# First input pieces on one DMA queue, blocks on two queues, 12 warming matmuls; indexer queries of the second chunk stacked by head pairs

## The chip, the cores and the metric

The kernel runs on one core of one Trainium2 chip. The metric is the device time of one execution in microseconds (us). The kernel before has a median of 431.6 us over 3 runs (431.47 to 431.8).

## The reference, cut to what matters

The kernel computes one step of a hybrid encoder layer for 256 prompt frames and 32 sample frames, 288 columns in all. Everything starts from one combined projection `p = x @ w_in`. The part that the second half of the change touches is the indexer of the sparse attention:

```
sc    = einsum('bqhd,bsd->bqhs', qi, ki) * IDX_DIM**-0.5      # 8 heads of 64, one shared key per frame
score = einsum('bqh,bqhs->bqs', wi * IDX_HEADS**-0.5, relu(sc))
adm   = arange(S) < (qpos // CHUNK + 1) * CHUNK               # CHUNK = 64: chunk-causal
score = where(adm, score, -inf)
_, idx = top_k(score, k_sel)                                  # k_sel = 64 for the 256 prompt frames
```

A prompt query in chunk 0 (frames 0 to 63) may use 64 keys, all of which it takes; one in chunk 1 (64 to 127) may use 128 keys; those in chunks 2 and 3 (128 to 255) up to 256 keys. Scores are thus needed for queries 64 to 127 against keys 0 to 127, and for queries 128 to 255 against keys 0 to 255.

## The kernel before, in words

Each projection tile is 128 output rows times 288 columns, summed over 8 blocks of 128 input rows. Every float32 operand is split into a high part (a cast to fp32r on ScalarE, `act.copy`) and a low part (a subtraction on VectorE), and each product is three fp32r matmuls: high by high, high by low, low by high.

The opening works block by block. The array `first` holds, for each input block k from 0 to 7, the 288 columns of x and the 128 weight columns of each of the first five tiles (0: the small tile with indexer key, gates and indexer weights; 1 to 4: the indexer queries): 928 columns, 464 KB. Block 0 is loaded in two pieces: `lead[0][:, 0:416]` (x and tile 0) on the queue of SP (line 161), the other 512 columns on the queue of ACT (line 162); blocks 1 to 7 follow on SP (line 164). For each block ACT casts `xh` (line 169) and `wh` (line 176), DVE subtracts `xl` (line 172) and `wl` (line 177). PE goes through the blocks in order (`first_products`, line 937): for block 0 three matmuls of tile 0, then 12 of tiles 1 to 4 with 224 columns each; for every later block 15, the first five of which need `wh` of that block. Ahead of them PE runs `WARM` = 18 matmuls on a zeroed tile (line 148), whose results nobody uses.

After the opening PE runs one tile after another (lines 899 to 901, 24 matmuls each), and a list of generators puts side work into the middle of each tile. ACT casts a tile's weights three tiles ahead, DVE subtracts two tiles ahead. All orders are fixed when the program is built; at run time engines only wait for semaphores.

The indexer queries of head pair j arrive as one tile of 128 rows (head 2j in rows 0 to 63, head 2j+1 in rows 64 to 127). `evac_qi` (lines 374 to 382) builds from them, for each head, a stationary operand `qst[:, h]` of 128 rows: high parts in the head's own half of the rows, low parts in the other half; `kih` and `kil` hold the key twice, so that one matmul with `kih` and one with `kil` give the full product. `index` (lines 384 to 404) then takes for each head queries 128 to 255 and queries 0 to 127, each against 256 keys, and ACT and DVE form relu and the weighted sum, with the weights `wn` (line 280).

Of the kernel before, what the change touches and what calls it, by code (L numbers as in the profile page):

```python
# [10 lines left out]
F32 = mybir.dt.float32  # L11
F32R = mybir.dt.float32r
BF = mybir.dt.bfloat16
AF = mybir.ActivationFunctionType
OP = mybir.AluOpType
# [5 lines left out]
TP = 256  # L21
TS = 32
T = TP + TS
KT = D // 128
AH, AD = 4, 256
BH, BD = 8, 128
IH, ID = 8, 64
CHUNK = 64
WARM = 18
MID = 4  # L30
FIRST = 5
LEAD = T + 128 * FIRST
# [8 lines left out]
NOT_ADMISSIBLE = -3.0e38  # L41
# [42 lines left out]
def body(ctx, tc, a, o):  # L84
    nc = tc.nc
    pe, act, dve, pool, sp = nc.tensor, nc.scalar, nc.vector, nc.gpsimd, nc.sync
# [5 lines left out]
    def sb(name, shape, dt=F32, tag=None, bufs=1):  # L92
        return P.tile(shape, dt, name=name, tag=tag or name, bufs=bufs)

    def bank(name, n=512):
        return ps.tile([128, 512], F32, name=name, tag="side", bufs=6)
# [24 lines left out]
    def pair(name):  # L121
        return (sb(f"wh{name}", [128, KT * 128], F32R, tag="wh", bufs=4),
                sb(f"wl{name}", [128, KT * 128], F32R, tag="wl", bufs=4))
# [18 lines left out]
    warm = sb("warm", [128, 256], BF)  # L142
# [3 lines left out]
    def keep_warm(n):  # L146
        for _ in range(n):
            pe.matmul(wp[:, :256], lhsT=warm[:, :128], rhs=warm, start=True, stop=True)

    keep_warm(WARM)  # L150

# [7 lines left out]
    lead = [sb(f"wst_k{k}", [128, KT * 128], tag="wst", bufs=8) for k in range(KT)]  # L159
    cut = T + 128  # L160
    sp.dma_start(lead[0][:, 0:cut], a["first"][:, 0, 0:cut])
    act.dma_start(lead[0][:, cut:LEAD], a["first"][:, 0, cut:])
    for k in range(1, KT):
        sp.dma_start(lead[k][:, 0:LEAD], a["first"][:, k])
    leads = []
    for k in range(KT):
        raw, (wh, wl) = lead[k], pair(f"_k{k}")
        leads.append((wh, wl))
        act.copy(xh[:, k], raw[:, 0:T])
        if k == 0:  # L170
            dve.tensor_copy(wh[:, 0:128], raw[:, T:cut])
        dve.tensor_tensor(xl[:, k], raw[:, 0:T], xh[:, k].bitcast(F32), OP.subtract)
        if k == 0:
            dve.tensor_tensor(wl[:, 0:128], raw[:, T:cut], wh[:, 0:128].bitcast(F32), OP.subtract)
        p = cut if k == 0 else T
        act.copy(wh[:, p - T:LEAD - T], raw[:, p:LEAD])
        dve.tensor_tensor(wl[:, p - T:LEAD - T], raw[:, p:LEAD], wh[:, p - T:LEAD - T].bitcast(F32), OP.subtract)
# [60 lines left out]
    start(8, bias_table())  # L238


    wn = sb("wn", [128, 3, 8])
    ws = sb("ws", [128, 2])
    gnat = sb("gnat", [128, 2, 3, 4])
    gns = sb("gns", [128, 3])
# [27 lines left out]
    def index_weights():  # L272
        sm = store["sm"]
        p = bank("wn_p")
        for b in range(2):
            pe.transpose(p[:, 128 * b:128 * b + 128], sm[:, 128 * b:128 * b + 128], ident)
        pe.transpose(p[:TS, 256:384], sm[:, TP:T], ident)
        c8 = float(np.float32(IH ** -0.5))
        for b in range(2):
            dve.tensor_scalar(wn[:, b], p[:, 128 * b + 68:128 * b + 76], c8, ID ** -0.5, op0=OP.mult, op1=OP.mult)  # L280
        dve.tensor_scalar(wn[:TS, 2], p[:TS, 256 + 68:256 + 76], c8, ID ** -0.5, op0=OP.mult, op1=OP.mult)
        yield
        for i in range(4):
            dve.tensor_copy(ws[32 * i:32 * i + 32], wn[:TS, 2, 2 * i:2 * i + 2])

    def gates():
        ig, z = store["ig"], store["z"]
# [77 lines left out]
            yield  # L365


    qst = sb("qst", [128, IH, TP], F32R, tag="cv")
    qis = sb("qis", [128, 4, TS])
    pool.memset(qst[:, :, 0:CHUNK].bitcast(F32), 0.0)  # L370
    kih = sb("kih", [128, TP], F32R, tag="hn", bufs=2)
    kil = sb("kil", [128, TP], F32R, tag="hn", bufs=2)

    def evac_qi(j, p):
        act.copy(qis[:, j], p[:, TP:T])
        new = slice(CHUNK, TP)
        half = (slice(0, 64), slice(64, 128))
        for e in range(2):
            act.copy(qst[half[e], 2 * j + e, new], p[half[e], new])
        for e in range(2):  # L380
            own, other, h = half[e], half[1 - e], 2 * j + e
            dve.tensor_tensor(qst[other, h, new], p[own, new], qst[own, h, new].bitcast(F32), OP.subtract)

    def index():
        acc = sb("acc", [128, 384], tag="sw", bufs=2)
        accs = sb("accs", [128, T], tag="sw", bufs=2)
        srel = [sb(f"srel{i}", [128, T], tag="ba", bufs=2) for i in range(2)]
        for j in range(IH // 2):
            p = [bank(f"ix{j}{e}") for e in range(2)]
            for e in range(2):  # L390
                h = 2 * j + e
                for c, q in ((0, slice(128, 256)), (256, slice(0, 128))):
                    pe.matmul(p[e][:, c:c + 256], lhsT=qst[:, h, q], rhs=kih, start=True, stop=False)  # L393
                    pe.matmul(p[e][:, c:c + 256], lhsT=qst[:, h, q], rhs=kil, start=False, stop=True)  # L394
            for e in range(2):
                h = 2 * j + e
                r = sb(f"r{h}", [128, 384], tag="lg", bufs=3)
                act.activation(r, p[e][:, :384], AF.Relu)
                w0, w1 = wn[:, 0, h:h + 1], wn[:, 1, h:h + 1]
                for c, w in ((slice(0, 256), w1), (slice(256, 384), w0)):  # L400
                    if h == 0:
                        dve.tensor_scalar(acc[:, c], r[:, c], w, None, op0=OP.mult)
                    else:
                        dve.scalar_tensor_tensor(acc[:, c], r[:, c], w, acc[:, c], op0=OP.mult, op1=OP.add)
            yield
            if j == 1:
                q = [bank(f"ixs{par}") for par in range(2)]
                for part in range(2):
                    for par in range(2):
                        r = slice(64 * par, 64 * par + 64)  # L410
                        c, keys = ((slice(0, 256), cki[r]), (slice(256, T), kiT[r, TP:T]))[part]
                        for i in range(4):
                            pe.matmul(q[par][32 * i:32 * i + 32, c], lhsT=qis[r, i], rhs=keys, start=True, stop=True)
                for par in range(2):
                    dve.tensor_scalar(srel[par], q[par][:, :T], 0.0, ws[:, par:par + 1], op0=OP.max, op1=OP.mult)
                dve.tensor_tensor(srel[0], srel[0], srel[1], OP.add)
            if j == 2:
                p = bank("ixsum")
                pe.matmul(p[:, :T], lhsT=stack, rhs=srel[0], start=True, stop=True)
                act.copy(accs, p[:, :T])  # L420
            yield
        dve.memset(acc[0:64, 256 + 64:384], NOT_ADMISSIBLE)
        dve.memset(acc[0:64, 192:256], NOT_ADMISSIBLE)
        top = sb("top", [128, 3, 8])
        for r in range(9):
            if r % 2:
                yield
            for i, (w, rows) in enumerate(((acc[:, 256:384], 128), (acc[:, 0:256], 128), (accs, 128))):
                if r == 8 and i < 2:
                    continue  # L430
                tt = top[:rows, i]
                dve.max(tt, w)
                dve.match_replace(w, tt, w, TAKEN)
            yield
        bm = store["bm"]
        dve.memset(acc[0:64, 256:256 + 64], TAKEN)
        mk = sb("mk", [128, 384], tag="lg", bufs=3)
        mks = srel[0]
        dve.tensor_scalar(mk, acc, TAKEN_LIMIT, MASK, op0=OP.is_gt, op1=OP.mult)
        dve.tensor_scalar(mks, accs, TAKEN_LIMIT, MASK, op0=OP.is_gt, op1=OP.mult)  # L440
        yield
        for h in range(0, 8, 2):
            dve.tensor_tensor(bm[:, h:h + 2], bm[:, h:h + 2], mk[:, None, :].to_broadcast([128, 2, 384]), OP.add)
            if h % 4 == 0:
                yield
        dve.tensor_tensor(bms, bms, mks[:, None, :].to_broadcast([128, 2, T]), OP.add)
        store["masked"] = True
# [7 lines left out]
    cv = sb("cv", [128, 2, D], tag="cv")  # L455
# [353 lines left out]
    def evac(t, p):  # L809
# [4 lines left out]
        if n == "sm":  # L814
            evac_small(p)
        elif n == "qi":
            evac_qi(j, p)
        elif n == "qb":
            act.copy(qbT[:, j], q)
# [208 lines left out]


    start(FIRST + 3, index())  # L1030
    s0 = POS["vb", 7] + 4
    start(s0 - 2, attn_sample())
# [18 lines left out]
    first = first_products()  # L1051
# [115 lines left out]
```

## Time and profile before

| what | value |
|---|---|
| median of 3 runs | 431.6 us |
| the profiled execution, its own time | 431.44 us |
| its span, first to last instruction | 429.7 us |
| PE busy | 422.5 us, 98% of the span |
| DVE busy | 299.2 us, 70% |
| ACT busy | 231.3 us, 54% |
| DMA, mean over the span | 183 GB/s |

The span leaves out 1.74 us of the execution's own time. A share of busy time is an average over stages; the opening, in which PE waits for data, is 1% of the span.

### The profile page before, as it was taken

The page shows a single profiled execution, that of the slowest core. Times are in us where ns is not written, and L with a number is a line of the kernel's source. Part 1 is how long each engine was busy: PE and PEld are TensorE (multiplying, and loading weights), DVE is VectorE, ACT ScalarE, POOL GpSimd, SP SyncE. Part 2 cuts the span into 40 slices and gives each one's busy share as a digit, 9 for nine tenths or more (in the row PEclk, how much of TensorE's full clock was granted, in tenths as well). Part 3 has the DMA queues.
Part 4 walks back from the last instruction along what each step waited for, and adds up shares of the span by engine and source line. Part 5 has one row for each costly group of instructions (what it writes and reads, how often), then busy time and mean ns, then how long its engine had stood idle before and what let it go on. Part 6 is the DMA issues. An engine that isn't in the chain of part 4 may idle for free.

```text
span 429.7 us, 8392 instructions
## 1 busy us (share of the span) xinstructions
PE 422.5 (98%) x3297; PEld 411.5 (96%) x3297; DVE 299.2 (70%) x598; ACT 231.3 (54%) x463; POOL 22.8 (5%) x44
## 2 busy tenths in 40 slices
PE   8999999999999999999999999999999999999994
PEld 7999999999999999999999999999999999998874
DVE  5779889886656664766999887776453465665674
ACT  6776456446665665557795465555433444446402
POOL 1000000000300000000001101101000000000031
PEclk9999999999999999999999999999999999999998
DMA  8986869968844455734454455554565558543014
GB/s 306 352 333 190 277 204 337 299 134 298 298 118 147 143 149 149 243 104 146 145 148 149 130 176 187 146 148 141 164 186 151 170 171 262 152 138 122 27 47 138
DMA packets 28707, 78.70 MB, mean 183 GB/s; under 512 B 7508, under 2 KB 10812, under 8 KB 27868
## 3 DMA queue, kind: packets, MB, share of 16 engines
q1 hardware_dynamic: 27804, 76.85, 57.4%
q10 hardware_dynamic: 864, 1.32, 0.9%
q8 instruction: 26, 0.43, 0.4%
q14 instruction: 13, 0.11, 0.1%
HBM read 72.39 MB, written 7.67 MB: 186 GB/s over the span
## 4 chain that ended last, share of the span: by engine, by line
PE 95%; DVE 2%; ACT 1%; DMA 1%; POOLq 0%; issue 0%; DVEq 0%; ACTq 0%
PE pj L900 25%; PE pj L899 25%; PE pj L901 25%; PE yn L918 5%; PE pj L937 3%; PE yn L922 1%; DMA wst_k<-in_first 1%; PE apt L569 1%; ACT wh L130 0%; PE al L550 0%; PE ix L394 0%; PE ix L393 0%; PE s L610 0%; PE av L579 0%; PE vt L623 0%; PE kt L664 0%
## 5 line engine op out<-in xcount | busy, mean ns | idle before, releaser
L899 PE MATMUL pj<-xh,wh 128*128 128x288 f32 x704 | 209.9, 298 | 0.1
L900 PE MATMUL pj<-xl,wh 128*128 128x288 f32 x704 | 207.7, 295 | 0.0
L901 PE MATMUL pj<-xh,wl 128*128 128x288 f32 x704 | 207.5, 295 | 0.0
L130 ACT CAST wh<-wst 128x1024 fp32r<-128x1024 f32 x112 | 117.8, 1052 | 132.3 <-PE pj L900 85.6
L137 DVE TENSOR_TENSOR wl<-wst,wh 128x1024 fp32r<-128x1024 f32 x112 | 136.4, 1219 | 32.3 <-ACT wh L130 31.9
L899 PEld LDWEIGHTS pj<-xh,wh 128*128 128x128 f32 x704 | 132.4, 188 | 0.9 <-issue 0.4
L900 PEld LDWEIGHTS pj<-xl,wh 128*128 128x128 f32 x704 | 132.4, 188 | 0.1
L901 PEld LDWEIGHTS pj<-xh,wl 128*128 128x128 f32 x704 | 132.3, 188 | 0.0
L899 PE MATMUL pj<-bbh,wh 128*128 128x288 f32 x64 | 19.1, 299 | 0.0
L900 PE MATMUL pj<-bbl,wh 128*128 128x288 f32 x64 | 19.0, 296 | 0.0
L900 PE MATMUL pj<-bal,wh 128*128 128x288 f32 x64 | 18.9, 295 | 0.0
L901 PE MATMUL pj<-bah,wl 128*128 128x288 f32 x64 | 18.9, 295 | 0.0
L901 PE MATMUL pj<-bbh,wl 128*128 128x288 f32 x64 | 18.8, 294 | 0.0
L899 PE MATMUL pj<-bah,wh 128*128 128x288 f32 x64 | 18.8, 293 | 0.0
L918 PE MATMUL yn<-wh,mxh 128*128 128x512 f32 x32 | 13.0, 407 | 0.0
L918 PE MATMUL yn<-wl,mxh 128*128 128x512 f32 x32 | 12.7, 396 | 0.1
L918 PE MATMUL yn<-wh,mxl 128*128 128x512 f32 x32 | 12.6, 394 | 0.0
L899 PEld LDWEIGHTS pj<-bbh,wh 128*128 128x128 f32 x64 | 12.1, 188 | 0.0
L901 PEld LDWEIGHTS pj<-bbh,wl 128*128 128x128 f32 x64 | 12.0, 188 | 0.0
L899 PEld LDWEIGHTS pj<-bah,wh 128*128 128x128 f32 x64 | 12.0, 188 | 0.0
L900 PEld LDWEIGHTS pj<-bal,wh 128*128 128x128 f32 x64 | 12.0, 188 | 0.0
L901 PEld LDWEIGHTS pj<-bah,wl 128*128 128x128 f32 x64 | 12.0, 188 | 0.0
(466 smaller groups left out, 567.8 us busy)
## 6 DMA issues: line engine op xcount, KB each, us to landing
wst<-in_w SPq DMA_DIRECT2D x112, 512.0 KB, 3.7
wst_k<-in_first SPq DMA_DIRECT2D x7, 464.0 KB, 4.8
rscr<-rrow SPq DMA_DIRECT2D x2, 768.0 KB, 6.8
out_k<-kbT SPq DMA_DIRECT2D x1, 1152.0 KB, 8.1
stC<-in_state_C SPq DMA_DIRECT2D x1, 1028.0 KB
out_C_sample<-stC SPq DMA_DIRECT2D x1, 1028.0 KB
bm<-rscr SPq DMA_DIRECT2D x1, 1024.0 KB, 7.6
ckT<-in_cache_k SPq DMA_DIRECT2D x1, 1024.0 KB
```

The lines of the kernel that those rows point to most:

```text
L130: act.copy(split[t][0], stage[t])
L137: dve.tensor_tensor(wl, stage[t], wh.bitcast(F32), OP.subtract)
L569: pe.transpose(p[:, 128 * i:128 * i + 128], lg[:, c:c + 128], ident)
L899: pe.matmul(p[:, :T], lhsT=wh[:, c], rhs=h[:, k], start=(k == 0), stop=False)
L900: pe.matmul(p[:, :T], lhsT=wh[:, c], rhs=l[:, k], start=False, stop=False)
L901: pe.matmul(p[:, :T], lhsT=wl[:, c], rhs=h[:, k], start=False, stop=(k == KT - 1))
L918: pe.matmul(p, lhsT=x[:, k, r], rhs=w[:, c], start=first and i == 0, stop=last and i == 2)
L922: pe.matmul(p[32 * q:32 * q + 32, 0:256], lhsT=lazy["mxs"][:, k], rhs=stage[t][:, 256 * q:256 * q + 256], start=first, stop=last)
L937: pe.matmul(p[t][:, new], lhsT=w[:, 128 * t:128 * t + 128], rhs=x[:, k, new], start=(k == 0 and w is wh and x is xh), stop=(k == KT - 1 an ...
```

## The change

In the opening, the second piece of block 0 moves from ACT's queue to SP's, right behind the first piece. Blocks 1, 3, 5 and 7 stay on SP; blocks 2, 4 and 6 go to ACT's queue: 2 and 4 behind a one-column copy named `tick`, 6 behind the cast of `xh` of block 1. The warming matmuls are 12 instead of 18.

In the indexer, a pair of heads now shares one stationary operand for the queries of chunk 1: `qst[:, j]` holds 128 columns for head 2j (queries 128 to 255), 128 columns with queries 64 to 127 of both heads side by side, and 128 columns for head 2j+1. The shared operand goes against keys 0 to 127 only. Its output rows 0 to 63 belong to head 2j, rows 64 to 127 to head 2j+1; they are weighted with `wp0` and the two halves are added at the end through the tile `odd`.

```diff
-WARM = 18
+WARM = 12
...
     sp.dma_start(lead[0][:, 0:cut], a["first"][:, 0, 0:cut])
-    act.dma_start(lead[0][:, cut:LEAD], a["first"][:, 0, cut:])
-    for k in range(1, KT):
-        sp.dma_start(lead[k][:, 0:LEAD], a["first"][:, k])
+    sp.dma_start(lead[0][:, cut:LEAD], a["first"][:, 0, cut:])
+    act.copy(sb("tick", [128, 1], BF), warm[:, 0:1])
+
+    def lead_load(q, k):
+        q.dma_start(lead[k][:, 0:LEAD], a["first"][:, k])
+
+    for k in (1, 3, 5, 7):
+        lead_load(sp, k)
+    for k in (2, 4):
+        lead_load(act, k)
...
+        if k == 1:
+            lead_load(act, 6)
         p = cut if k == 0 else T
         act.copy(wh[:, p - T:LEAD - T], raw[:, p:LEAD])
...
-        for b in range(2):
-            dve.tensor_scalar(wn[:, b], p[:, 128 * b + 68:128 * b + 76], c8, ID ** -0.5, op0=OP.mult, op1=OP.mult)
-        dve.tensor_scalar(wn[:TS, 2], p[:TS, 256 + 68:256 + 76], c8, ID ** -0.5, op0=OP.mult, op1=OP.mult)
+        dve.tensor_scalar(wn[:, 0], p[:, 128 + 68:128 + 76], c8, ID ** -0.5, op0=OP.mult, op1=OP.mult)
+        dve.tensor_scalar(wn[:TS, 1], p[:TS, 256 + 68:256 + 76], c8, ID ** -0.5, op0=OP.mult, op1=OP.mult)
+        for e in range(2):
+            dve.tensor_scalar(wp0[64 * e:64 * e + 64], p[64:128, 68 + e:76:2], c8, ID ** -0.5, op0=OP.mult, op1=OP.mult)
...
-    qst = sb("qst", [128, IH, TP], F32R, tag="cv")
+    qst = sb("qst", [128, IH // 2, 384], F32R, tag="cv")
-    pool.memset(qst[:, :, 0:CHUNK].bitcast(F32), 0.0)
...
-        for e in range(2):
-            act.copy(qst[half[e], 2 * j + e, new], p[half[e], new])
-        for e in range(2):
-            own, other, h = half[e], half[1 - e], 2 * j + e
-            dve.tensor_tensor(qst[other, h, new], p[own, new], qst[own, h, new].bitcast(F32), OP.subtract)
+        parts = [(e, slice(t0, t1), slice(c, c + t1 - t0))
+                 for e, t0, t1, c in ((0, 64, 128, 128), (0, 128, 256, 0), (1, 64, 256, 192))]
+        for e, new, c in parts:
+            act.copy(qst[half[e], j, c], p[half[e], new])
+        for e, new, c in parts:
+            own, other = half[e], half[1 - e]
+            dve.tensor_tensor(qst[other, j, c], p[own, new], qst[own, j, c].bitcast(F32), OP.subtract)
...
+            both = p[1][:, 256:384]
+            for k in (kih, kil):
+                pe.matmul(both, lhsT=qst[:, j, 128:256], rhs=k[:, 0:128],
+                          start=(k is kih), stop=(k is kil))
+            for e in range(2):
+                for k in (kih, kil):
+                    pe.matmul(p[e][:, 0:256], lhsT=qst[:, j, 256 * e:256 * e + 128], rhs=k, start=(k is kih), stop=(k is kil))
             for e in range(2):
                 h = 2 * j + e
-                for c, q in ((0, slice(128, 256)), (256, slice(0, 128))):
-                    pe.matmul(p[e][:, c:c + 256], lhsT=qst[:, h, q], rhs=kih, start=True, stop=False)
-                    pe.matmul(p[e][:, c:c + 256], lhsT=qst[:, h, q], rhs=kil, start=False, stop=True)
-            for e in range(2):
-                h = 2 * j + e
+                n = 256 + 128 * e
                 r = sb(f"r{h}", [128, 384], tag="lg", bufs=3)
-                act.activation(r, p[e][:, :384], AF.Relu)
+                act.activation(r[:, :n], p[e][:, :n], AF.Relu)
...
+        odd = sb("odd", [128, 384], tag="lg", bufs=3)
+        dve.tensor_copy(odd[64:128, 0:128], acc[0:64, 256:384])
+        dve.tensor_tensor(acc[64:128, 256:384], acc[64:128, 256:384], odd[64:128, 0:128], OP.add)
```

On ACT the program begins before as follows. `wst_k_90` to `wst_k_97` are blocks 0 to 7 there; `xh` and `wh_k` are the high parts of x and of the weights.

```order
L162 DMA wst_k_90<-in_first 128x512
L169 ACT_TABLE_LOAD
L169 CAST xh<-wst_k_90 128x288
L176 CAST wh_k_107<-wst_k_90 128x512
L169 CAST xh<-wst_k_91 128x288
L176 CAST wh_k_115<-wst_k_91 128x640
```

Now it begins as follows; `wst_k_84` to `wst_k_91` are blocks 0 to 7 here.

```order
L163 ACT_TABLE_LOAD
L163 COPY tick<-warm 128x1
L166 DMA wst_k_86<-in_first 128x928
L166 DMA wst_k_88<-in_first 128x928
L176 CAST xh<-wst_k_84 128x288
L185 CAST wh_k_102<-wst_k_84 128x512
L176 CAST xh<-wst_k_85 128x288
L166 DMA wst_k_90<-in_first 128x928
L185 CAST wh_k_110<-wst_k_85 128x640
```

The table load and the copy `tick` moved ahead of ACT's DMA issues, which are now blocks 2 and 4, and block 6 stands behind the cast of x of block 1.

On SP the program begins before with these issues (same names):

```order
L161 DMA wst_k_90<-in_first 128x416
L164 DMA wst_k_91<-in_first 128x928
L164 DMA wst_k_92<-in_first 128x928
L164 DMA wst_k_93<-in_first 128x928
L164 DMA wst_k_94<-in_first 128x928
```

and now with these:

```order
L161 DMA wst_k_84<-in_first 128x416
L162 DMA wst_k_84<-in_first 128x512
L166 DMA wst_k_85<-in_first 128x928
L166 DMA wst_k_87<-in_first 128x928
L166 DMA wst_k_89<-in_first 128x928
L166 DMA wst_k_91<-in_first 128x928
```

Block 1 now has both pieces of block 0 ahead of it on its queue instead of one.

On PE the first pair of heads of the indexer stands in the middle of a tile; `ix_515` and `ix_516` are the two output banks before, `kih` and `kil` the high and low parts of the key:

```order
L393 MATMUL ix_515<-kih,qst 128x256
L394 MATMUL ix_515<-kil,qst 128x256
L393 MATMUL ix_515<-kih,qst 128x256
L394 MATMUL ix_515<-kil,qst 128x256
L393 MATMUL ix_516<-kih,qst 128x256
L394 MATMUL ix_516<-kil,qst 128x256
L393 MATMUL ix_516<-kih,qst 128x256
L394 MATMUL ix_516<-kil,qst 128x256
```

and now, with the banks `ix_520` and `ix_521`:

```order
L403 MATMUL ix_521<-kih,qst 128x128
L403 MATMUL ix_521<-kil,qst 128x128
L407 MATMUL ix_520<-kih,qst 128x256
L407 MATMUL ix_520<-kil,qst 128x256
L407 MATMUL ix_521<-kih,qst 128x256
L407 MATMUL ix_521<-kil,qst 128x256
```

Eight matmuls of 256 columns became four of 256 and two of 128; there are four such groups, one for each pair of heads.

## Rows read from the trace of the kernel before

**Rows 1.** The page, busy time of each engine (share of the span) and instructions.

```profile
PE 422.5 (98%) x3297; PEld 411.5 (96%) x3297; DVE 299.2 (70%) x598; ACT 231.3 (54%) x463; POOL 22.8 (5%) x44
```

**Rows 2.** Waits of PE: who waited for whom, total us, times, longest us.

```profile
PE pj L937 <- ACT xh L169: 0.2, 1, 0.2
```

**Rows 3.** Timeline of PE, 4.6 to 9 us: start, duration, instruction, count.

```profile
4.89 0.40 PE L937 MATMUL pj<-xh,wh_k 128*128 128x288 f32 x1 [0.22 <-ACT xh L169]
...
5.82 0.60 PE L937 MATMUL pj<-xh,wh_k 128*128 128x224 f32 x4
...
7.15 0.74 PE L937 MATMUL pj<-xh,wh_k 128*128 128x288 f32 x5
```

**Rows 4.** Timeline of ACT, 4 to 9.4 us.

```profile
4.41 0.43 ACT L169 CAST xh<-wst_k 128x288 fp32r<-128x288 f32 x1 [1.89 <-DMA wst_k<-in_first]
...
5.70 0.43 ACT L169 CAST xh<-wst_k 128x288 fp32r<-128x288 f32 x1 [0.34 <-DMA wst_k<-in_first]
6.04 0.72 ACT L176 CAST wh_k<-wst_k 128x640 fp32r<-128x640 f32 x1
6.91 0.44 ACT L169 CAST xh<-wst_k 128x288 fp32r<-128x288 f32 x1
...
8.11 0.43 ACT L169 CAST xh<-wst_k 128x288 fp32r<-128x288 f32 x1
...
9.32 0.43 ACT L169 CAST xh<-wst_k 128x288 fp32r<-128x288 f32 x1
```

**Rows 5.** Timeline of all engines, 0 to 12 us: the first issues.

```profile
0.80 0.41 ACTq L162 DMA_DIRECT2D wst_k<-in_first  x1
...
0.81 0.39 SPq L161 DMA_DIRECT2D wst_k<-in_first  x1
0.90 0.17 DVE L143 MEMSET warm<- 128x128 uint32 x1 [0.90 <-PEq L1145]
...
1.24 1.28 ACT L169 ACT_TABLE_LOAD   x1 [1.24 <-PEq L1145]
```

**Rows 6.** DMA queues, 3.2 to 3.6 us: packets, MB, share; q1 SP's, q10 ACT's.

```profile
q10 hardware_dynamic: 44, 0.09, 58.8%
q1 hardware_dynamic: 43, 0.07, 47.2%
```

**Rows 7.** Busy time by stretch; the last two columns are DMA share and GB/s.

```profile
3.60:4.00 0.40, 0.40 (x4) 0.28 (x2) 0.00 (x0) 0.00 (x0) 0.00 (x0) 1.00 1.12 426
4.40:5.70 1.30, 0.98 (x6) 0.49 (x4) 1.05 (x4) 0.95 (x2) 0.00 (x0) 1.00 1.04 423
```

**Rows 8.** Timeline of ACT, 199.75 to 200.2 us.

```profile
198.56 1.28 ACT L847 ACT_TABLE_LOAD   x1
...
200.16 0.37 ACT L580 COPY qbT<-av 128x256 f32<-128x256 f32 x1
```

**Rows 9.** Line 130, 199.5 to 200 us: duration ns min/median/max, first and last start.

```profile
L130 ACTq EVENT_SEMAPHORE  x1: 1462/1462/1462, 199.8 to 199.8; - x1
```

**Rows 10.** Chain of waits in order of time, at 31 and at 139 us.

```profile
30.93 0.12 PE ix L393
...
31.87 0.13 PE pj L899
...
139.12 0.33 PE apt L569 x3
```

**Rows 11.** Busy time, 19.2 to 60 us: PE, PEld, DVE, ACT, POOL.

```profile
19.20:60.00 40.80, 40.80 (x340) 40.35 (x339) 33.09 (x67) 25.98 (x58) 0.00 (x0) 1.00 0.77 250
```

**Rows 12.** Tile qst: duration ns min/median/max, first and last start.

```profile
L382 DVE TENSOR_TENSOR qst<-pj,qst x8: 350/356/361, 20.3 to 31.8; 64x192 fp32r<-64x192 f32 x8
```

**Rows 13.** Timeline of PE, the warming matmuls, at 1.2 to 2.2 and 4.2 to 4.3 us.

```profile
1.12 1.46 PE L148 MATMUL warm_p<-warm 128*128 128x256 bf16 x6 [1.12 <-DVE warm L143]
...
3.87 0.69 PE L148 MATMUL warm_p<-warm 128*128 128x256 bf16 x4
```

**Rows 14.** Busy time near the end; the column of 1.00 is the granted clock.

```profile
424.00:427.00 3.00, 0.06 (x1) 0.00 (x0) 0.59 (x1) 0.37 (x1) 0.00 (x0) 1.00 1.02 290
```

More of the change, by code (lines that the diff above doesn't have):

```diff
@@ L238, in body @@
     start(8, bias_table())
-    wn = sb("wn", [128, 3, 8])
+    wn = sb("wn", [128, 2, 8])
+    wp0 = sb("wp0", [128, 4])
     ws = sb("ws", [128, 2])
@@ L278, in index_weights @@
         c8 = float(np.float32(IH ** -0.5))
-        for b in range(2):
-            dve.tensor_scalar(wn[:, b], p[:, 128 * b + 68:128 * b + 76], c8, ID ** -0.5, op0=OP.mult, op1=OP.mult)
-        dve.tensor_scalar(wn[:TS, 2], p[:TS, 256 + 68:256 + 76], c8, ID ** -0.5, op0=OP.mult, op1=OP.mult)
+        dve.tensor_scalar(wn[:, 0], p[:, 128 + 68:128 + 76], c8, ID ** -0.5, op0=OP.mult, op1=OP.mult)
+        dve.tensor_scalar(wn[:TS, 1], p[:TS, 256 + 68:256 + 76], c8, ID ** -0.5, op0=OP.mult, op1=OP.mult)
+        for e in range(2):
+            dve.tensor_scalar(wp0[64 * e:64 * e + 64], p[64:128, 68 + e:76:2], c8, ID ** -0.5, op0=OP.mult, op1=OP.mult)
         yield
         for i in range(4):
-            dve.tensor_copy(ws[32 * i:32 * i + 32], wn[:TS, 2, 2 * i:2 * i + 2])
+            dve.tensor_copy(ws[32 * i:32 * i + 32], wn[:TS, 1, 2 * i:2 * i + 2])
     def gates():
@@ L375, in evac_qi @@
         act.copy(qis[:, j], p[:, TP:T])
-        new = slice(CHUNK, TP)
         half = (slice(0, 64), slice(64, 128))
-        for e in range(2):
-            act.copy(qst[half[e], 2 * j + e, new], p[half[e], new])
-        for e in range(2):
-            own, other, h = half[e], half[1 - e], 2 * j + e
-            dve.tensor_tensor(qst[other, h, new], p[own, new], qst[own, h, new].bitcast(F32), OP.subtract)
+        parts = [(e, slice(t0, t1), slice(c, c + t1 - t0))
[5 more added lines that the diff above has]
+            dve.tensor_tensor(qst[other, j, c], p[own, new], qst[own, j, c].bitcast(F32), OP.subtract)
     def index():
@@ L389, in index @@
             p = [bank(f"ix{j}{e}") for e in range(2)]
+            both = p[1][:, 256:384]
[5 more added lines that the diff above has]
+                    pe.matmul(p[e][:, 0:256], lhsT=qst[:, j, 256 * e:256 * e + 128], rhs=k, start=(k is kih), stop=(k is kil))
             for e in range(2):
                 h = 2 * j + e
-                for c, q in ((0, slice(128, 256)), (256, slice(0, 128))):
-                    pe.matmul(p[e][:, c:c + 256], lhsT=qst[:, h, q], rhs=kih, start=True, stop=False)
-                    pe.matmul(p[e][:, c:c + 256], lhsT=qst[:, h, q], rhs=kil, start=False, stop=True)
-            for e in range(2):
-                h = 2 * j + e
+                n = 256 + 128 * e
                 r = sb(f"r{h}", [128, 384], tag="lg", bufs=3)
-                act.activation(r, p[e][:, :384], AF.Relu)
-                w0, w1 = wn[:, 0, h:h + 1], wn[:, 1, h:h + 1]
-                for c, w in ((slice(0, 256), w1), (slice(256, 384), w0)):
-                    if h == 0:
+                act.activation(r[:, :n], p[e][:, :n], AF.Relu)
+                for c, w in ((slice(0, 256), wn[:, 0, h:h + 1]), (slice(256, 384), wp0[:, j:j + 1]))[:1 + e]:
+                    if j == 0 and (e == 0 or c.start):
                         dve.tensor_scalar(acc[:, c], r[:, c], w, None, op0=OP.mult)
@@ L421, in index @@
             yield
-        dve.memset(acc[0:64, 256 + 64:384], NOT_ADMISSIBLE)
+        odd = sb("odd", [128, 384], tag="lg", bufs=3)
+        dve.tensor_copy(odd[64:128, 0:128], acc[0:64, 256:384])
+        dve.tensor_tensor(acc[64:128, 256:384], acc[64:128, 256:384], odd[64:128, 0:128], OP.add)
         dve.memset(acc[0:64, 192:256], NOT_ADMISSIBLE)
@@ L436, in index @@
         dve.memset(acc[0:64, 256:256 + 64], TAKEN)
+        dve.memset(acc[0:64, 256 + 64:384], NOT_ADMISSIBLE)
         mk = sb("mk", [128, 384], tag="lg", bufs=3)
```

## The prediction

> **What bounds the kernel now.** I read the page first: PE is busy 98% of the span [rows 1]. Then the waits of PE: beside the start, its only wait of any size is 0.2 us for the first cast of x [rows 2]. So PE sets the end, and a change counts by two things: what it takes from PE's own work, and how it moves the moments at which PE's fixed order has to stand still. The second is possible only in the opening. From the opening's rows of PE [rows 3] and of ACT [rows 4] the reader is to see how closely they follow each other: the first piece of block 0 is there at 4.41, ACT casts 0.43 us, and PE starts at 4.89, 0.05 after. Tiles 1 to 4 of block 0 run from 5.82 to 7.15, then block 1 starts at once. Its cast of x began at 5.70, that of its weights lasts from 6.04 to 6.76, so PE could have had block 1 at 6.81: 0.34 us of slack. After that ACT's casts come every 1.2 us (5.70, 6.91, 8.11, 9.32), while PE needs three groups of five matmuls for a block, some 1.74 us; data gets further ahead with every block. Block 1 is the tight place, and the place on which this change turns.
>
> **The opening: which bytes are ahead of block 1.** Before, SP carries 208 KB (first piece) and then the blocks, ACT's queue 256 KB (the rest of block 0). When block 1 has landed, 208 + 256 + 464 = 928 KB have moved; each further block costs 1.2 us, which is 464 KB (475,136 bytes) at 394 GB/s [rows 4]. Both queues are served evenly while both have work: from 3.2 to 3.6 ACT's moves 44 packets, SP's 43 [rows 6]. Together they move 426 GB/s; one queue alone moves 423 [rows 7]. So a second queue shares the bandwidth and hardly adds any.
>
> The Trainium skill says so too, in its main page, Trainium Kernel Development and Optimization, section Key Constraints: queues of several engines run on the same DMA engines and interleave, and issuing from several only saves issue time. The trace agrees by the 426 and 423 just named; by this rule the two queues of the change bring nothing that pays for what they put ahead of block 1.
>
> After the change SP has 208 + 256 + 464 KB up to block 1, three DMAs of 128 rows, and ACT's queue has blocks 2 and 4, two such DMAs of larger rows. Served one packet each in turn, ACT's two blocks are through before SP's third DMA is, provided they start early. Do they? `tick` waits for DVE's memset, which ends at 0.90 + 0.17 = 1.07; before, the table load stood at 1.24 behind the DMA issue of 0.41 [rows 5], now it is first and would end near 2.1. Does a DMA issue wait until the table load and the copy have run? At 199.8 ACT's sequencer was already at a semaphore instruction [rows 9] that stands in its program behind the copy of line 580, which ran at 200.16, and behind a table load from 198.56 to 199.84 [rows 8]. So it runs ahead of its engine and stops only for semaphores. I take it that blocks 2 and 4 are issued from 1.1 on, 0.3 us later than ACT's piece before.
>
> Then block 1 lands when 208 + 256 + 3 x 464 = 1,856 KB have moved, which before was the moment of block 3: 8.11 [rows 4]. At 426 instead of 394 GB/s the three blocks would be 0.27 us faster; I take 8.0, since it is open how much of that is overlap at the edges of a stretch. From the cast of x to PE are 6.81 - 5.70 = 1.11 us, so block 1 starts on PE at 9.1 instead of 7.15: **+1.95 us**. Bounds: if only block 2 is ahead, 6.91 + 1.11 = 8.02, +0.87; if block 6 too, 9.32 + 1.11 = 10.43, +3.3 (it stands behind the cast of x of block 1, which waits, so I don't expect it); below, the slack of 0.34 us is all that an earlier start could win, since 928 KB have to land before block 1 in any order. The first piece itself gains nothing on this path: PE may start earlier or later than 4.89, it waits for block 1 anyway. Low parts follow: DVE's subtraction for block 1 comes under the first ten of its matmuls as now. All later blocks are ahead again: block 2 is there before block 1, block 3 follows on SP some 1.2 us after it.
>
> Nothing gives this time back, since PE doesn't stand still anywhere behind: it is busy 40.80 of 40.80 us from 19.2 to 60 [rows 11].
>
> The warming matmuls cost nothing by themselves; six fewer free PE when it has no data. What depends on them is the clock: see the rivals.
>
> **The indexer on PE.** A pair of heads takes from 30.93 to 31.87, 0.94 us for 8 matmuls of 256 columns, 0.1175 each [rows 10]. Four stay: 0.47. Two of 128 columns come in; no fp32r matmul of that width is in the trace. The nearest rows: the 224-column ones of the opening, 12 in 1.33 us, 0.11 each [rows 3], and transposes of 128 columns in plain float32, 0.33 for three, 0.11 each [rows 10]. Fewer columns don't get under 0.11 there, so I take 0.11. A pair then costs 0.69, four pairs save 4 x 0.25 = **1.0 us**. Bounds: if the short form cost as much as two of those float32 steps, 0.22 each, the saving is 4 x 0.03 = 0.1 us; if it went with the columns, 0.06 each, it is 1.4 us.
>
> **ACT and DVE around it.** Each head pair has one more cast and one more subtraction, smaller ones; the weights one more tiny operation; the weighted sum has 12 operations instead of 16; a copy and an addition come before the top-8 search; POOL loses a memset. I cost all this at nothing: PE is never waiting from 19.2 to 60, with DVE busy 33.09 and ACT 25.98 of 40.80 us [rows 11]. Without that cover, four casts and four subtractions of at most 0.36 us [rows 12] would be 2.9 us.
>
> **The sum**, against the profiled execution's own time of 431.44 (span 429.7 and 1.74 around it; 0.16 below the median of 431.6): 431.44 + 1.95 - 1.0 = 432.4 us.
>
> **Rivals.** (a) ACT's issues do wait for the table load and `tick`, to 2.1 us or later. Then the first piece is alone, and block 2 with only part of block 4 is ahead of block 1: from +0.87 upward, say +1.0 to +1.3. For it: no row shows a DMA issue that passes work of its own engine. Against it: [rows 8, 9]. It gives 431.3 to 431.8, no change.
>
> (b) The clock comes late. 256 columns take (1.46 - 0.42)/5 = 0.21 us at the start, the 1.2 GHz level, where 0.42 is the duration of one; from 3.87 on the spacing falls to 0.11, the 2.4 GHz level [rows 13]. PE had worked without a pause since 1.12. With 12 warming matmuls it stops near 3.7, just before that, and has next to nothing until data is there. For it: the pause lies where the clock rose. Against it: at the end the granted clock stayed at 1.00 through 3 us in which PE did 0.06 us of work [rows 14], so one pause need not undo what came before. If it rises only while PE is at work on block 1, block 0 (12 matmuls, 1.33) and part of block 1 take twice their time; half of the former hides in waits: some +0.9 us, 433.3. The Trainium skill, TensorE: Matmul & The Clock Gate, Part 1, says that the slow clock is the default and sustained activity releases it, which speaks for this case.
>
> (c) The short fp32r matmul saves nothing (bound above): 431.44 + 1.95 - 0.1 = 433.3.
>
> (d) The other side: block 1 isn't held up, because ACT's queue starts its blocks only after SP has moved block 1, or yields to SP. Its place is PE's start of block 1; it decides if that start is at 7.15 or before. Price: 0 to -0.34 from the opening and -1.0 from the indexer, 430.1 to 430.4, faster. Against it: the even service in [rows 6].
>
> **Chances.** Forecast 0.50, (a) 0.22, (b) 0.12, (c) 0.06, (d) 0.10. About 0.2%, 0.86 us, is what a measurement of this kernel can tell from no change. The forecast's own range, 431.9 to 433.0, straddles the line at 432.4: half of it counts as slower, 0.25, and half as no change. Slower: 0.25 + 0.12 + 0.06 = 0.43. No change: 0.25 + (a), less a little for (a) with a larger saving: 0.44. Faster: (d) and that little, 0.13. The range for 8 of 10 reaches to (d) and, upward, past (b) and (c) toward the bound of +3.3: 430.5 to 433.6.
>
> **What would show it.** Right: ACT's issues of blocks 2 and 4 start near 1.1 and 1.6; ACT's cast of x of block 1 starts near 8.0, PE's first 128x288 group of five near 9.1, with PE waiting for ACT ahead of it; ACT's queue shows 0.93 MB moved before that. The indexer's six matmuls take 0.69 us, and PE stays without waits from 22 us on. Wrong: the issues start after 2.1 (a); 224-column matmuls of block 0 are spaced 0.19 or more (b); the six take 0.9 us (c); PE reaches block 1 at 7.15 or earlier (d). A wait of PE for `acc`, `qst` or a tile's low part after 20 us would break the term that I cost at nothing.

## The result, and the profile after

The changed kernel takes 437.48 us (median of 4 runs, 436.48 to 438.82), the kernel before 431.70 beside it: a ratio of 1.0136, 95% interval 1.0121 to 1.0151. It is slower by 5.8 us; the forecast was +0.8 and its range ended at 433.6. The profiled execution took 436.48 (span 434.7), 5.04 more than the one of before; it is the shortest of the four, and the only one with a trace.

PE is still busy 98% of a longer span (the line below, as in [rows 1]). Its waits (who waited for whom, total us, times, longest) have a new one, in the opening, in place of the 0.2 us of [rows 2]:

```profile
PE 425.7 (98%) x3283; PEld 414.1 (95%) x3283; DVE 299.1 (69%) x601; ACT 230.7 (53%) x468; POOL 22.3 (5%) x43
```

```profile
PE warm_p L148 <- DVE warm L143: 1.1, 1, 1.1
PE pj L953 <- ACT wh_k L185: 1.1, 1, 1.1
```

The timeline of ACT in the opening (start, duration, instruction, count, idle time before it and what ended it) answers to [rows 4, 5]:

```profile
0.81 1.28 ACT L163 ACT_TABLE_LOAD   x1 [0.81 <-PEq L1161]
1.11 0.90 ACTq L166 DMA_DIRECT2D wst_k<-in_first  x2
2.10 0.19 ACT L163 COPY tick<-warm 128x1 bf16<-128x1 bf16 x1
3.50 0.43 ACT L176 CAST xh<-wst_k 128x288 fp32r<-128x288 f32 x1 [1.20 <-DMA wst_k<-in_first]
5.71 0.62 ACT L185 CAST wh_k<-wst_k 128x512 fp32r<-128x512 f32 x1 [1.78 <-DMA wst_k<-in_first]
8.12 0.43 ACT L176 CAST xh<-wst_k 128x288 fp32r<-128x288 f32 x1 [1.79 <-DMA wst_k<-in_first]
8.13 0.34 ACTq L166 DMA_DIRECT2D wst_k<-in_first  x1
```

ACT issues blocks 2 and 4 at 1.11, during the table load and ahead of `tick`. The first piece of block 0 lands 0.9 us earlier than before, the second 1.1 us later (its last completion is at 5.69 instead of 4.56), block 1 2.4 us later; ACT casts it from 8.12 on. PE in the same stretch, against [rows 3]:

```profile
3.98 0.61 PE L953 MATMUL pj<-xh,wh_k 128*128 128x288 f32 x1
...
6.38 1.19 PE L953 MATMUL pj<-xh,wh_k 128*128 128x224 f32 x4 [1.06 <-ACT wh_k L185]
7.37 1.05 PE L953 MATMUL pj<-xl,wh_k 128*128 128x224 f32 x4
8.22 1.05 PE L953 MATMUL pj<-xh,wl_k 128*128 128x224 f32 x4
9.28 1.27 PE L953 MATMUL pj<-xh,wh_k 128*128 128x288 f32 x5
10.38 0.74 PE L953 MATMUL pj<-xl,wh_k 128*128 128x288 f32 x5
```

Four matmuls of 224 columns begin 0.85 us apart from the next four (7.37 to 8.22), where before it was some 0.44; from 10.38 a group of five of 288 takes 0.74 as before. So block 0 and the start of block 1 ran at the 1.2 GHz level. Block 1 begins at 9.28, without a wait in the list: at this clock block 0 lasts nearly until block 1 is there.

The six matmuls of the first head pair take from 33.51 to 34.20:

```profile
33.51 0.22 PE L403 MATMUL ix<-kih,qst 128*128 128x128 f32 x1
33.56 0.28 PE L403 MATMUL ix<-kil,qst 128*128 128x128 f32 x1
33.68 0.34 PE L407 MATMUL ix<-kih,qst 128*128 128x256 f32 x1
...
34.09 0.28 PE L407 MATMUL ix<-kil,qst 128*128 128x256 f32 x1
34.20 0.30 PE L915 MATMUL pj<-xh,wh 128*128 128x288 f32 x1
```

To divide the rest I read three starts from the timeline of PE: A, the first matmul of the tiles behind the opening; the 240th tile matmul after it, behind the indexer; and B, the first of the last product `yn`. The last column runs from the start of the last `yn` matmul to the end of the span.

| us | A | 240th | B | B - A | last `yn` to the end |
|---|---|---|---|---|---|
| before | 19.32 | 57.48 | 389.89 | 370.57 | 10.44 |
| after | 21.96 | 59.37 | 393.91 | 371.95 | 11.45 |

The opening has lost 2.64 us. The end is 1.0 us longer. In the kernels below it lasts 10.2 to 10.8 us with the old indexer and 10.5 to 11.1 with the new one (one trace each, means 10.5 and 10.9), so some 0.4 us of this may belong to the indexer's part; the rest I count as the execution's own. Neither is shown. But B - A should have shrunk by the indexer's 1.0 us, and it grew by 1.4. Nothing waits there: PE is busy 40.10 of 40.10 us from 21.9 to 62 (start:end, us, then PE, PEld, DVE, ACT, POOL), as in [rows 11].

```profile
21.90:62.00 40.10, 40.10 (x332) 39.65 (x332) 32.77 (x68) 25.16 (x61) 0.00 (x0) 1.00 0.72 229
```

The page's costliest groups name it (busy us and mean ns of one behind the bar), before and after:

```profile
L899 PE MATMUL pj<-xh,wh 128*128 128x288 f32 x704 | 209.9, 298 | 0.1
L900 PE MATMUL pj<-xl,wh 128*128 128x288 f32 x704 | 207.7, 295 | 0.0
L901 PE MATMUL pj<-xh,wl 128*128 128x288 f32 x704 | 207.5, 295 | 0.0
```

```profile
L915 PE MATMUL pj<-xh,wh 128*128 128x288 f32 x704 | 211.2, 300 | 0.0
L917 PE MATMUL pj<-xh,wl 128*128 128x288 f32 x704 | 209.0, 297 | 0.0
L916 PE MATMUL pj<-xl,wh 128*128 128x288 f32 x704 | 208.4, 296 | 0.0
```

The same 2112 matmuls, of the same shape and operands, are each 1 to 2 ns longer: from one start to the next, gaps left out, the mean over them is 133.38 instead of 132.26 ns, and 133.31 instead of 132.34 over all 2496 tile matmuls between A and B. No instruction of them was changed. What was changed is where their weights lie: the tile `tick`, two bytes per partition, is allotted 32 between the staging buffers and the weight buffers, and in the built program these begin at byte 70368 of a partition instead of 70336.

### The profile page after: what moved, and what is told of

It is laid out like the page before. It is cut to its first block, busy times and chain, and to the rows that moved or that the text cites. A ratio compares the mean times of both kernels' runs of the same rounds, so it can differ in the third digit from the quotient of the medians.

```text
span 434.7 us, 8370 instructions
## 1 busy us (share of the span) xinstructions
PE 425.7 (98%) x3283; PEld 414.1 (95%) x3283; DVE 299.1 (69%) x601; ACT 230.7 (53%) x468; POOL 22.3 (5%) x43
## 4 chain that ended last, share of the span: by engine, by line
PE 96%; DMA 1%; ACT 1%; DVE 0%; ACTq 0%; issue 0%; SPq 0%
PE pj L915 26%; PE pj L917 26%; PE pj L916 25%; PE yn L934 5%; PE pj L953 4%; DMA wst_k<-in_first 1%; PE yn L938 1%; PE apt L585 1%; PE ix L407 0%; PE al L566 0%; PE c L697 0%; PE s L626 0%; PE av L595 0%; PE ht L663 0%; PE vbn L485 0%; PE kt L680 0%
## 5 line engine op out<-in xcount | busy, mean ns | idle before, releaser
L700 ACT COPY oc_all<-c 128x257 f32<-128x257 f32 x8 | 2.9, 376 | 17.3 <-PE c L699 17.3
L916 PEld LDWEIGHTS pj<-bbl,wh 128*128 128x128 f32 x64 | 12.1, 188 | 0.0
```

Of the source, the lines that this page charges most:

```text
L700: act.copy(oc[:, kd], p[:, :257])
L916: pe.matmul(p[:, :T], lhsT=wh[:, c], rhs=l[:, k], start=False, stop=False)
```

## The experiments

These are all twelve. "Ratio" is to the kernel before on the same chip, with its 95% interval; the last columns are as in the table above, the last one B - A less that of before.

| kernel | median us | ratio | A | B - A, change |
|---|---|---|---|---|
| pad32 | 434.13 | 1.0057 [1.0045, 1.0069] | 19.22 | +2.57 |
| pad64 | 433.43 | 1.0042 [1.0029, 1.0055] | 19.45 | +1.76 |
| pad96 | 431.61 | 1.0001 [0.9992, 1.0011] | 19.31 | -0.06 |
| front32 | 431.51 | 0.9997 [0.9988, 1.0006] | 19.28 | -0.05 |
| after_tick128 | 434.61 | 1.0066 [1.0053, 1.0078] | 23.08 | -1.16 |
| index_only | 430.97 | 0.9984 [0.9976, 0.9993] | 20.05 | -1.00 |
| opening_only | 434.40 | 1.0061 [1.0049, 1.0073] | 23.71 | -0.16 |
| warm12 | 432.85 | 1.0022 [1.0008, 1.0036] | 22.20 | 0.00 |
| after_w18 | 432.83 | 1.0027 [1.0017, 1.0037] | 21.29 | -1.15 |
| one_queue | 432.67 | 1.0035 [1.0020, 1.0050] | 21.21 | -0.95 |
| late_act | 436.35 | 1.0098 [1.0074, 1.0122] | 25.22 | -0.95 |
| k1_on_act | 433.28 | 1.0030 [1.0017, 1.0043] | 20.17 | -0.95 |

The two parts are told apart by the columns: what was done to the opening shows in A, what was done to the indexer or the buffers' places in B - A.

### Buffers' places

**pad32.** To the kernel before, behind SP's issues of the blocks:

```diff
+    sb("spacer", [128, 8])
```

> The kernel before with one unused tile of 32 bytes per partition between the staging buffers and the weight buffers, nothing else. The placement theory: in the changed kernel the new two-byte tile tick moves everything behind it by 32 bytes (the weight buffers from byte 70336 to 70368), and that makes each of the 2112 matmuls of 288 columns about 0.97 ns longer; so this kernel is 2112 x 0.97 ns = 2.0 us slower than before (about 433.7), with the mean spacing of these matmuls at 133.3 ns instead of 132.3. The rival, that the slower matmuls come with the changed opening or the indexer, or are chance of that execution: 0.0 us, spacing 132.3 ns.

+2.57 us in B - A, and the median agrees. The groups of the page are those of the changed kernel to 0.3 us:

```profile
L900 PE MATMUL pj<-xh,wh 128*128 128x288 f32 x704 | 211.2, 300 | 0.0
L902 PE MATMUL pj<-xh,wl 128*128 128x288 f32 x704 | 209.0, 297 | 0.0
L901 PE MATMUL pj<-xl,wh 128*128 128x288 f32 x704 | 208.7, 296 | 0.0
```

A tile that nothing reads or writes costs 2.6 us. The rival falls.

**after_tick128.** To the changed kernel:

```diff
-    act.copy(sb("tick", [128, 1], BF), warm[:, 0:1])
+    act.copy(sb("tick", [128, 64], BF)[:, 0:1], warm[:, 0:1])
```

> The changed kernel with tick as a tile of 128 bytes per partition, so that all behind it is moved by 128 bytes instead of 32. The placement theory: the matmuls go back to 132.3 ns, 2.0 us come off the changed kernel's 437.5, so about 435.5, +3.8 against before. The rival (the slow matmuls belong to the rest of the change): no difference to the changed kernel, about 437.5.

B - A falls from 371.95 to 369.41, 2.54 us, and the median from 1.0136 to 1.0066 of before. The theory holds from both sides.

**pad64, pad96, front32.** The spacer of pad32 with 16 or 24 columns instead of 8, or with 8 columns ahead of `xh` (and so ahead of all the buffers named here) instead of behind the staging buffers.

> The kernel before with an unused tile of 64 bytes per partition in the place of the spacer of 32: what stands behind is moved by 64 bytes. If it is the remainder by 64 bytes that counts (weights from byte 70336 to 70400, both multiples of 64), the matmuls stay at 132.3 ns and the time at 431.6, within 0.2. If any move away from the old places costs, up to +2.6 us as with 32 bytes.

> The kernel before with an unused tile of 96 bytes in the place of the spacer: the weight buffers from byte 70432. With +32 the 1408 matmuls of xh and xl with wh and wl cost about 1.0 to 1.8 ns more each, with +64 about 0.9 ns, and the changed kernel with +128 cost nothing there. If the places repeat every 128 bytes and the old one alone is good: +1.5 to +2.6 us, 433.1 to 434.2. If +96 is as good as +128: 431.6.

> The kernel before with the unused tile of 32 bytes ahead of xh, so that xh, xl, the staging buffers and the weights all move by 32 bytes and keep their distances. If the distance between the moving operand and the weights decides: 431.6, within 0.3. If the place of the weights alone decides, as with the spacer of 32 behind the staging buffers: +2.6 us, about 434.1.

pad64 costs 1.76 us: that a multiple of 64 bytes would do was wrong. pad96 costs nothing, and front32 nothing: there the weights lie at byte 70368, as in pad32, but `xh` and `xl` have moved with them, and the groups are those of before again:

```profile
L900 PE MATMUL pj<-xh,wh 128*128 128x288 f32 x704 | 210.0, 298 | 0.1
L901 PE MATMUL pj<-xl,wh 128*128 128x288 f32 x704 | 207.6, 295 | 0.0
L902 PE MATMUL pj<-xh,wl 128*128 128x288 f32 x704 | 207.5, 295 | 0.0
```

So it isn't the address of the weights by itself that counts but how it stands to the buffers ahead of them. Which of these is not shown: front32 moved the moving operands `xh` and `xl` and the staging buffers together. That the moving operand alone decides doesn't fit other lines of the same pages. `bbh` and `bbl`, the moving operands of eight late tiles, lie behind the weights and moved with them in pad32 and in front32 alike; yet in pad32 two of their pairs change (before first, then pad32):

```profile
L900 PE MATMUL pj<-bbl,wh 128*128 128x288 f32 x64 | 19.0, 296 | 0.0
L901 PE MATMUL pj<-bbh,wl 128*128 128x288 f32 x64 | 18.8, 294 | 0.0
```

```profile
L902 PE MATMUL pj<-bbh,wl 128*128 128x288 f32 x64 | 19.0, 297 | 0.0
L901 PE MATMUL pj<-bbl,wh 128*128 128x288 f32 x64 | 18.8, 294 | 0.0
```

In front32 they take 296 and 294 ns again. For the weights against the buffers ahead of them, +0, +96 and +128 bytes were good on the whole, +32 and +64 bad. A period of 128 bytes would fit these five; other distances weren't tried, and in pad96 one pair (`xl`, `wh`) is faster and another (`xh`, `wh`) slower than before, so the rule is more than this.

### The indexer alone

**index_only.** The changed kernel's `index_weights`, `evac_qi` and `index` with the opening of before. The edit, to the changed kernel:

```diff
-WARM = 12
+WARM = 18
...
-    sp.dma_start(lead[0][:, cut:LEAD], a["first"][:, 0, cut:])
-    act.copy(sb("tick", [128, 1], BF), warm[:, 0:1])
...
-    for k in (1, 3, 5, 7):
-        lead_load(sp, k)
-    for k in (2, 4):
-        lead_load(act, k)
+    act.dma_start(lead[0][:, cut:LEAD], a["first"][:, 0, cut:])
+    for k in range(1, KT):
+        sp.dma_start(lead[k][:, 0:LEAD], a["first"][:, k])
...
-        if k == 1:
-            lead_load(act, 6)
```

> The kernel before with only the indexer's part of the change; its opening, 18 warming matmuls and the buffers' places are those of before. By the trace of the changed kernel (the shift falls from 2.52 to 1.89 us over the indexer): -0.6 to -0.7 us, about 431.0; by the prediction's term -1.0, about 430.7. The rival, that the slow matmuls come from the indexer's new buffers: +2.0 - 0.7 = +1.3 us, about 433.0.

B - A falls by 1.00 us, and by 0.95 to 1.16 in all the other kernels with the new indexer and good places. The median shows -0.6 (interval -1.0 to -0.3). In the profiled execution (431.40) the rest went to the clock: with the opening and the 18 warming matmuls of before, its first matmuls ran at the lower level until 7 us, and A is 20.05. That this holds for the median is not shown. The kernel is faster than both others, and the best of the study.

### The opening

**opening_only.** The reverse, with `tick` at 128 bytes. The edit is the opening's part of the change, as shown in its diff.

> The kernel before with only the opening's part of the change (two pieces of block 0 on SP's queue, blocks 2, 4 and 6 on ACT's, 12 warming matmuls), with tick at 128 bytes. By the shift of the first tile behind the opening in the changed kernel: +2.64 us, about 434.3, and up to +3.6 if the 1.0 us at the end of the execution belongs to the change. By the prediction's term for the opening (+1.95): 433.6. If the slow matmuls belonged to the opening whatever the buffers' places: +4.6, about 436.3.

+2.8 in the median, near the first number; A is 4.4 us late in the profiled execution, the longest of the six, and far more than in the changed kernel. The stretches say why (the third number from the end is the granted clock):

```profile
4.00:5.00 1.00, 0.91 (x3) 0.53 (x3) 0.61 (x2) 0.00 (x0) 0.00 (x0) 1.00 1.02 398
5.00:6.00 1.00, 0.07 (x1) 0.00 (x0) 0.00 (x0) 0.40 (x1) 0.00 (x0) 1.00 1.03 419
...
7.00:8.00 1.00, 1.00 (x8) 1.00 (x7) 0.00 (x0) 0.00 (x0) 0.00 (x0) 0.61 1.06 408
8.00:9.00 1.00, 0.34 (x2) 0.07 (x1) 0.46 (x1) 0.97 (x2) 0.00 (x0) 0.50 0.98 375
...
14.00:15.00 1.00, 1.00 (x10) 1.00 (x10) 0.82 (x2) 0.79 (x2) 0.00 (x0) 0.97 1.01 401
```

Here the clock had risen and fell again to 1.2 GHz at some 7.3 us, after PE had stood still for 1.21 us, with 0.07 us of work from 5 to 6 us; it came back at 14. Matmuls that are ready in between run at half speed.

**warm12, after_w18.** The number of warming matmuls alone: 12 in the kernel before, 18 in after_tick128.

```diff
-WARM = 18
+WARM = 12
```

> The kernel before with 12 warming matmuls instead of 18, nothing else. The clock theory: warming ends at 3.9 us, PE has nothing until 4.9, and blocks 0 and 1 then run at half clock, so the first tile behind the opening starts 0.5 to 1.5 us later: 432.1 to 433.1. The rival, that in the changed kernel only the late blocks cost and the number of warming matmuls is indifferent: 431.6.

> The changed kernel with tick at 128 bytes and 18 warming matmuls instead of 12. If 12 were too few: the matmuls of block 0 and 1 run at full speed, the first tile starts at 21.1 to 21.9 instead of 23.1 us, and the time is 433.0 to 433.4 instead of 434.6. If the gap of about 1 us before the second piece of block 0 takes the clock whatever the warming: no difference, 434.6. In both cases block 1 still starts at 9.1 us, because its data lands then.

warm12 costs 1.2 us in the median, with runs from 431.2 (nothing lost) to 434.1; in the profiled one, the longest, block 1 starts at 8.65 and its first two groups take 1.29, where 0.74 is full speed:

```profile
6.95 1.05 PE L937 MATMUL pj<-xl,wh_k 128*128 128x224 f32 x4
...
8.65 1.29 PE L937 MATMUL pj<-xh,wh_k 128*128 128x288 f32 x5
9.75 1.29 PE L937 MATMUL pj<-xl,wh_k 128*128 128x288 f32 x5
```

after_w18 wins 1.7 us on after_tick128 (ratios 1.0066 and 1.0027), and its eight runs lie within 0.9 us. PE runs at full speed and stands still twice:

```profile
6.13 0.70 PE L953 MATMUL pj<-xh,wh_k 128*128 128x224 f32 x4 [0.86 <-ACT wh_k L185]
...
9.03 0.84 PE L953 MATMUL pj<-xh,wh_k 128*128 128x288 f32 x5 [1.30 <-ACT wh_k L185]
```

So the lower clock of the changed kernel comes with the six matmuls that were taken out, and not from the gap before block 0's second piece: that gap is here too. But 18 don't always do: index_only shows the lower level at the start with as many. With the clock up, A is 1.98 us late. This is the price of the loads' order alone.

**one_queue, late_act, k1_on_act.** Three attempts at that order, all with the new indexer, 18 warming matmuls and the places of before (without `tick`); the diffs show the loads alone. one_queue has everything on SP's queue; late_act issues 2, 4 and 6 on ACT's queue behind the casts of `xh` of blocks 0, 1 and 2; k1_on_act is one_queue with block 1 on ACT's queue.

```diff
# one_queue, to the changed kernel
-    for k in (1, 3, 5, 7):
+    for k in range(1, KT):
         lead_load(sp, k)
-    for k in (2, 4):
-        lead_load(act, k)
...
-        if k == 1:
-            lead_load(act, 6)
# late_act, to the changed kernel
-    for k in (2, 4):
-        lead_load(act, k)
...
-        if k == 1:
-            lead_load(act, 6)
+        if k < 3:
+            lead_load(act, 2 * k + 2)
# k1_on_act, to one_queue
+    act.dma_start(lead[1][:, 0:LEAD], a["first"][:, 1])
     sp.dma_start(lead[0][:, cut:LEAD], a["first"][:, 0, cut:])
...
-    for k in range(1, KT):
+    for k in range(2, KT):
```

> The indexer's part of the change, block 0 in two pieces on SP's queue and the blocks 1 to 7 behind them on the same queue in their order, ACT's queue empty, 18 warming matmuls, buffers at the places of before. If it is the blocks 2 and 4 on ACT's queue that hold block 1 up: the first piece lands by 3.5 us as in the changed kernel, block 1 is on PE at about 6.5 us instead of 7.15 (before) and 9.28 (changed), and with -0.95 for the indexer the time is about 430.0. If the split of block 0 on one queue is itself the delay (the second piece lands at 5.7 us as in the changed kernel): 432 or more.

> The changed kernel with 18 warming matmuls, without tick (buffers where they were before), and with ACT's issues of blocks 2, 4 and 6 behind its casts of xh of blocks 0, 1 and 2 instead of ahead of all: the indexer, the two pieces and SP's queue are those of the change. If blocks 2 and 4 ahead of block 1 are what holds it up: block 1 is cast at 5.0 to 6.0 us instead of 7.9, PE begins it at 6.5 to 7.0 instead of 9.0, and the time is 430.0 to 430.7. If three or more transfers on SP's queue are slow by themselves, as with one queue: block 1 at 7.4 us or later, 432.0 to 432.8.

> The kernel of one_queue with block 1 alone moved to ACT's queue (issued at 0.8 us, ahead of the table load); both pieces of block 0 and the blocks 2 to 7 on SP's. Block 1 then shares the DMA engines with block 0 from the start: 950 KB by about 5.2 us. If the trouble of one queue is a transfer behind others on the same queue: block 1 on PE at about 6.7 us, and with the indexer 430.0 to 430.6. If the two pieces lose as much as block 1 gains: about 431.0, as with the indexer alone.

All three miss the hope. In one_queue block 0 is complete at 4.01, earlier than in any other, and block 1 still comes at 7.84 (ACT's timeline):

```profile
3.37 0.43 ACT L173 CAST xh<-wst_k 128x288 fp32r<-128x288 f32 x1 [1.28 <-DMA wst_k<-in_first]
4.01 0.62 ACT L180 CAST wh_k<-wst_k 128x512 fp32r<-128x512 f32 x1 [0.22 <-DMA wst_k<-in_first]
7.84 0.43 ACT L173 CAST xh<-wst_k 128x288 fp32r<-128x288 f32 x1 [3.21 <-DMA wst_k<-in_first]
```

A transfer has sixteen completions in the trace. Read as one group for each transfer, 14 of block 1's came by 6.24 and the last two at 7.38 and 7.82; in the changed kernel they lie between 7.41 and 8.10, in the kernel before between 5.19 and 5.68. In late_act it is the same (13 by 6.24, then 7.39, 7.64, 7.86). Why two or three parts straggle where SP's queue is alone in its first microseconds stays open. late_act shows one thing more. Its block 2 was issued on ACT's queue at 3.28, when SP's queue had been given six transfers, and came only at 11.94; by the queues of 3.7 to 7.2 us and of 7.3 to 9.9, ACT's q10 moved nothing in the first stretch:

```profile
q1 hardware_dynamic: 295, 0.99, 88.2%
```

```profile
q1 hardware_dynamic: 185, 0.62, 59.2%
q10 hardware_dynamic: 119, 0.41, 39.4%
```

PE waited 2.05 us for that block, and then ran at a granted clock of 0.50 from 13.3 to 16.7 us; so late_act is the worst of the three.

k1_on_act lands the first piece at 4.92 and starts block 1 at 8.00, without a wait: now block 0 is what comes late. Its trace is of one of its shorter executions (431.96 of a median of 433.28); why most took longer is not shown. None of the openings beats that of before.

## Why the prediction was wrong

**Right: what stands ahead of block 1, +1.95.** ACT's issues came at 1.11, as read from [rows 8, 9]; the cast of block 1 at 8.12 (forecast 8.0), PE's start at 9.28 (9.1). With the clock up, after_w18 has A 1.98 us late. ACT's queue moved 0.95 MB before 8.12, the two blocks (the queues of 0 to 8.12 us):

```profile
q1 hardware_dynamic: 541, 1.36, 46.4%
q10 hardware_dynamic: 288, 0.95, 31.9%
```

Its reason was only nearly right. "Both queues are served evenly" holds where both were issued together [rows 6]. In the changed kernel the transfers end in the order of their issue: block 2 (issued at 1.11) is complete at 5.10, SP's second piece (1.25) at 5.69, block 4 (1.56) at 7.66, block 1 (1.71) at 8.10. From 3.1 to 3.9 us ACT's block 2, issued at 1.11, has the DMA engines to itself while SP's second piece, issued at 1.25, waits; late_act has the reverse.

```profile
q10 hardware_dynamic: 76, 0.28, 96.5%
q1 hardware_dynamic: 1, 0.00, 0.1%
```

The order isn't strict: from 5.5 to 6.5 us both queues move packets, 65 and 54. The sum came to the same, since ACT's two blocks are ahead of block 1 by either rule. Rivals (a) and (d) are out: the issues didn't wait, and block 1 was held up. But in one_queue, without ACT's blocks, block 1 is cast only 0.28 us earlier (7.84): the number came out, but that these blocks alone cost it is not shown.

**Right: the indexer, -1.0.** Six matmuls take 0.69 us, as worked out, and B - A is 1.00 less in index_only. That the sum came out so well is in part luck: the two of 128 columns take 0.17 instead of 0.22 (0.05 and 0.12, so the bound 0.06 was as near as the 0.11 that I took), and the four of 256 take 0.52 instead of 0.47. Rival (c) is out.

**Right: the edits of ACT and DVE at nothing.** PE waits for none of them behind the opening.

**Mis-sized: the clock, rival (b).** It was given 0.12 and +0.9 us. It happened, by its own test (224 columns spaced 0.21, where 0.19 was the sign), and is worth 1.7 us between after_tick128 and after_w18 (1.0066 and 1.0027 of 431.6), 1.2 in warm12, and 2.9 in its profiled execution (A at 22.20). The step that failed is the evidence against it, [rows 14]: that the clock stayed up through 3 us at the end in which PE hardly worked. The stretch was cut off too early; in the same trace the granted clock falls 0.3 us behind it:

```profile
427.30:428.00 0.70, 0.00 (x0) 0.00 (x0) 0.00 (x0) 0.00 (x0) 0.00 (x0) 0.50 0.12 44
```

So that row could not count against the rival. opening_only shows the clock fall within the opening after a shorter pause, and warm12 shows it rise too late. The price was too small because I let the clock rise while PE works on block 1, and let half of the loss hide in waits; in warm12 it stayed low through block 0 and into the third group of block 1 (1.07 us against 1.29), and nothing hid it. The Trainium skill, TensorE: Matmul & The Clock Gate, Part 1, which the prediction cited for this rival, also says that the number of slow matmuls at the start differs from run to run; warm12's runs from 431.2 to 434.1 fit that.

**Missing: a term for the buffers' places, +2.5 us.** This is the largest piece of the miss, and it failed in the step that took matmul durations of before for those of after: "Nothing gives this time back", and nothing was asked about what takes more. `tick` was counted as an instruction of ACT, not as 32 bytes ahead of every weight buffer. 2.54 us (after_tick128) over the 2496 matmuls of 288 columns between A and B are 1.0 ns each, the lengthening that the starts show; pad32 gives the same 2.57 without the rest of the change.

Together: forecast 432.4; the profiled execution adds 2.5 for the places, 0.7 for the opening (A at +2.64 instead of +1.95, most of it the clock) and 1.0 at the end of the span, less 0.15 by which B - A is shorter in opening_only and after_tick128 than the indexer explains: 436.45, measured 436.48. The median is 1.0 us longer than this execution, and nothing here accounts for that. By ratios: 1.0136 (changed), 1.0066 with the places mended, 1.0027 with 18 warming matmuls, 0.9984 with the old order of blocks.

## What to carry to other kernels

A new tile is an edit of every buffer allotted behind it: where PE sets the end, compare the addresses of the weights and of the buffers ahead of them before and after, and put small tiles last, or round them up (128 bytes cost nothing here, 64 did). Warming matmuls are sized by when data comes; those taken out between the start and the first product cost more than they seem, and not in every run, so look at several. When a change is three changes, price each by the column it can show in: here the good one (the indexer, -1 us) was hidden under two bad ones.

## What the runs showed of the hardware that was not expected

- The spacing of fp32r matmuls of 288 columns depends on how far the weights lie in memory from the buffers ahead of them, the moving operands `xh` and `xl` among these: 132.3 ns with the distance of before, and with 96 or 128 bytes more on the whole the same, 133.3 with 32 more. What in it decides stays open. The Trainium skill, TensorE: Matmul & The Clock Gate, Step-by-step: what each phase is for, says that TensorE reads moving operand and weights by two independent ports. By that alone the distance would not matter; the measurements differ, and they decide.
- With transfers on SP's queue alone from the start (one_queue, late_act), the last parts of block 1 came 1.1 to 1.6 us behind the rest, and the DMA engines moved 271 to 316 GB/s from 4 to 8 us in one_queue, where the kernel before has 394 to 422.
- The view by stretch gives the granted clock as 1.00 in the opening of the changed kernel from 2 to 9 us, where matmuls took twice their time; the durations are the better witness there.
